# HGRN value columns as one token-major product, with three smaller edits, in a two-layer trunk on one core

## The chip, the cores and the metric

The kernel runs on one core of a Trainium2 chip. The metric is the time on the device of one execution in microseconds (us), as the median of three runs. TensorE (PE) does matrix products and transposes, VectorE (DVE) and ScalarE (ACT) work on 128 partitions, GpSimd (POOL) does some element-wise work and issues the DMAs that add while they move, and SyncE (SP) issues most other DMAs. Each engine works through its own instructions in program order and waits on semaphores.

## The reference, cut to what matters

Two trunk layers run over 128 context tokens and 512 latent tokens, 640 in all, at a model width of 2048. Per layer:

```
shift, scale, gate = split(silu(cond) @ ada_w + ada_b)      # two conditioning vectors: context, latent
h = x * (1 + scale) + shift
z = h @ w_in        # 6656 columns: aq ak av ag | hq hi hff hfb hgate | ca cb cgate
A: windowed attention with a sink (8 heads of 128, 2 key heads), gated by silu(ag)
B: HGRN2, 4 heads of 128, both directions: q = silu(hq), v = hi, k and decay from hff / hfb,
   S_t = diag(f_t) S_{t-1} + k_t v_t^T, o_t = S_t^T q_t; RMS norm, times silu(hgate)
C: conv: ca * sigmoid(cb), 31 taps over positions, LayerNorm, silu, times silu(cgate)
x = LayerNorm(ALPHA * x + gate * (concat(A, B, C) @ w_out))
```

In B, `v` enters as a matrix with the tokens on its rows: it is the stationary or the moving operand of products that contract over tokens.

## The kernel before, in words

All 640 tokens stay on the core. The modulated stream lies in SBUF with channels on partitions, as 16 blocks (k tiles) of 128 channels by 5 blocks of 128 tokens, split into a high part `HH` and a low part `HL`. Each weight tile is split the same way into `wh` (hi, lo), and every product is a sum of three: hi by HH, hi by HL, lo by HH.

**Projection tiles.** `w_in` is cut into 52 tiles of 128 columns (`NTILES`). A tile's result, 128 columns by 640 tokens, lies channel-major in two PSUM banks `z`. Per k tile and product `mm` issues two matmuls that share their weights, one over 256 tokens (L1173) and one over 384 (L1175), so a tile has 48 such pairs. Two z tiles alternate, and a tile's PSUM must be read out (`zput`) before the next tile but one may start. In the main loop PE does a tile in eight half steps, and after each `pump` lets up to three of the waiting generators (`active`) take one step; a generator that cannot get a buffer steps aside. If no z tile is free when a tile is to start, `pump_until` runs generators, one step each, and no projection matmul is issued in between.

**HGRN.** For each head four tiles come in the order hff, hfb, hi, hq. `e_hi` copies the value tile to SBUF, transposes it on PE in five blocks (`to_tokens`, L474 and L478) and copies the result to `v`, which `hg_main` reads. `hg_main` runs beside the next tiles' matmuls: its last steps are the output matmuls (L693 to L697), two copies on ACT (L699, L700), a square on ACT (L708) and on DVE (L709, L710), a column sum on PE (`psum_part`, L426 and L427), logarithm and exponential on ACT (L716, L719) and a product on DVE (L721). The four hgate tiles follow the four heads, then ak, av and four aq tiles. `e_ak` (L754, L759) reads the key tile out of PSUM as soon as it has three of the nine buffers of the pool `S`, of which `hg_main` holds up to seven.

**Modulation products.** Layer 0's shift and scale are computed on PE at the start (`ada_pe`, L317 and L327, 64 weight tiles of 512 KB); as each pair of channel blocks is ready, `build_h0` makes the stream and `start_mm` does the first three projection tiles for those two k tiles. The other four vectors (`ada_dve`) are products on DVE (L362), each of 128x256 elements against a row of the conditioning vector that is broadcast by DMA (L352); `RATE` says how often they take a step in the main loop.

**Weights in the main loop.** SP loads a weight tile (L1120); ACT writes hi (L290) and minus hi (L291), and a POOL-issued DMA adds the weights once more to give lo (L292). This is `split_add`. Elsewhere `split` does it with two instructions on ACT or POOL and on DVE or POOL.

**Between the layers.** The output projection works in column groups of 512, 512, 512, 256 and 256 (L1431; the last one L1482). For the last group the five token blocks follow one another. Each is added to the residual and normalised (`ln_norm`, half of it on ACT), and `ln_next` transposes it on PE into the next layer's stream (L1384, four banks of PSUM in turn; 16 small ACT instructions L1391 per token block). Between these stand products of layer 1's first two tiles, over the first 256 tokens.

## Time and profile before

| | |
|---|---|
| median of 3 runs | 2241.97 us (2239.75 to 2242.38) |
| profiled execution | 2247.12 us, its span 2245.3 us |
| PE busy | 2177.4 us, 97% |
| DVE busy | 1457.9 us, 65% |
| ACT busy | 1144.7 us, 51% |
| POOL busy | 601.9 us, 27% |
| DMA | 403.61 MB, 180 GB/s over the span |

PE works nearly all the time, so the span is PE's work plus the places where it stands still. The start (to about 120 us) moves data at the highest rate of the span. Layer 0's projection runs to about 930 us, its output projection to about 1140 us, the change of layers to about 1200 us, and layer 1 follows in the same order.

### The profile page before, as it was taken

Reading aid. Unit: us, or ns where it says so; the run is one execution under the profiler, and the core shown is the slowest. Engines: PE = TensorE matmul, PEld = TensorE weight load, DVE = VectorE, ACT = ScalarE, POOL = GpSimd, SP = SyncE. Lnnn points to the kernel's source line nnn. Section 1 sums busy time; section 2 is a strip of 40 time slices with the busy share of each in tenths; the row PEclk is TensorE's granted clock in tenths of the full one; section 3 lists DMA queues with packets and bytes.
Section 4 is the critical chain, followed back from the end, with each engine's and each line's share of the span. In section 5 each row is a group of like instructions: output and inputs, shape, how many; then the busy total and the mean of one; then the engine's idle time right before and its main releaser. Section 6 shows DMA issues by size and latency. Waiting matters only on the chain.

```text
span 2245.3 us, 42128 instructions
## 1 busy us (share of the span) xinstructions
PE 2177.4 (97%) x15854; PEld 2076.1 (92%) x15854; DVE 1457.9 (65%) x3799; ACT 1144.7 (51%) x2051; POOL 601.9 (27%) x690
## 2 busy tenths in 40 slices
PE   5899999999999999999989999999999999999997
PEld 2699999999999999988989999999999999998887
DVE  2478899557669999766673666543654779225457
ACT  1267877546565435511155787774555543462112
POOL 0033344332222343300032344433222123331003
PEclk9999999999999999999999999999999999999999
DMA  9978787897766888964426777778776576676333
GB/s 358 392 206 199 185 209 182 201 219 173 176 159 155 206 193 212 259 233 128 128 108 158 156 172 162 162 173 189 160 163 137 110 173 147 150 164 212 99 99 123
DMA packets 210557, 403.61 MB, mean 180 GB/s; under 512 B 24656, under 2 KB 30512, under 8 KB 209712
## 3 DMA queue, kind: packets, MB, share of 16 engines
q1 hardware_dynamic: 138992, 271.85, 38.4%
q0 software_dynamic: 61440, 116.96, 30.2%
q10 hardware_dynamic: 9920, 12.10, 1.7%
q8 instruction: 124, 2.03, 0.4%
q14 instruction: 81, 0.66, 0.1%
HBM read 383.46 MB, written 12.11 MB: 176 GB/s over the span
## 4 chain that ended last, share of the span: by engine, by line
PE 75%; DVE 9%; DMA 6%; issue 5%; ACT 3%; POOL 1%; ACTq 1%; SPq 0%; POOLq 0%; DVEq 0%
PE z L1175 29%; PE z L1173 19%; PE z L1431 9%; PE m L1431 8%; DVE junk L362 4%; DMA x<-adaw 2%; PE m L948 2%; PE m L1482 2%; PE m L862 1%; DMA s<-xT 1%; PE m L916 1%; DMA s<-s 1%; DMA wh<-win 1%; PE m L664 1%; ACT s L1391 1%
## 5 line engine op out<-in xcount | busy, mean ns | idle before, releaser
L1175 PE MATMUL z<-HH,wh 128*128 128x384 f32 x3296 | 1046.6, 339 | 0.0
L1173 PE MATMUL z<-HH,wh 128*128 128x256 f32 x3296 | 926.6, 283 | 1.9 <-DMA wh<-win 1.0
L292 POOL DMA_DIRECT2D wh<-win x388 | 345.2, 936 | 1095.3 <-ACT wh L291 1024.0
L1173 PEld LDWEIGHTS z<-HH,wh 128*128 128x128 f32 x3296 | 619.5, 189 | 5.8 <-DVE wh L287 1.6
L1175 PEld LDWEIGHTS z<-HH,wh 128*128 128x128 f32 x3296 | 620.6, 188 | 1.5
L1175 PE MATMUL z<-HL,wh 128*128 128x384 f32 x1648 | 558.2, 339 | 0.0
L362 DVE SCALAR_TENSOR_TENSOR junk<-raw,s 128x256 bf16<-128x256 f32 x1024 | 502.5, 491 | 53.2 <-DMA raw<-adawD 25.0
L1173 PE MATMUL z<-HL,wh 128*128 128x256 f32 x1648 | 461.6, 280 | 0.0
L1173 PEld LDWEIGHTS z<-HL,wh 128*128 128x128 f32 x1648 | 310.9, 189 | 0.0
L1175 PEld LDWEIGHTS z<-HL,wh 128*128 128x128 f32 x1648 | 310.4, 188 | 0.0
L291 ACT ACTIVATE wh<-wh 128x512 fp32r<-128x512 f32 x400 | 253.0, 633 | 78.5 <-PE z L1175 67.4
L290 ACT CAST wh<-raw 128x512 fp32r<-128x512 f32 x400 | 244.0, 610 | 72.0 <-issue 36.1
L286 ACT CAST wh<-raw 128x512 fp32r<-128x512 f32 x136 | 83.0, 621 | 305.0 <-PE m L1431 153.8
L1027 DVE SCALAR_TENSOR_TENSOR s<-s,sm,s 128x655 f32<-128x655 f32 x240 | 229.6, 957 | 6.3
L1431 PE MATMUL z<-wh,HH 128*128 128x512 f32 (+1 forms) x640 | 182.1, 368 | 0.0
L1431 PE MATMUL m<-wh,HH 128*128 128x512 f32 (+1 forms) x640 | 173.8, 357 | 0.0
L287 DVE TENSOR_TENSOR wh<-raw,wh 128x512 fp32r<-128x512 f32 x138 | 92.6, 687 | 119.5 <-ACT wh L286 119.5
L1431 PEld LDWEIGHTS z<-wh,HH 128*128 128x128 f32 x640 | 116.1, 189 | 20.1
L1431 PEld LDWEIGHTS m<-wh,HH 128*128 128x128 f32 x640 | 114.2, 189 | 17.6
L1431 PE MATMUL z<-wh,HL 128*128 128x512 f32 (+1 forms) x320 | 117.8, 368 | 0.0
L1431 PE MATMUL m<-wh,HL 128*128 128x512 f32 (+1 forms) x320 | 114.4, 358 | 0.0
L1096 ACT ACTIVATE s<-z 128x640 f32<-128x640 f32 x32 | 22.5, 703 | 152.5 <-PE z L1175 143.7
(561 smaller groups left out, 2718.6 us busy)
## 6 DMA issues: line engine op xcount, KB each, us to landing
raw<-win SPq DMA_DIRECT2D x416, 256.0 KB, 4.2
wh<-win POOLq DMA_DIRECT2D x388, 256.0 KB, 5.6
raw<-adawD SPq DMA_DIRECT2D x256, 256.0 KB, 4.2
x<-adaw SPq DMA_DIRECT2D x64, 512.0 KB, 8.3
raw<-wout SPq DMA_DIRECT2D x128, 256.0 KB, 2.7
s<-crow SPq DMA_DIRECT2D x32, 256.0 KB, 5.9
s<-xT ACTq DMA_DIRECT2D x16, 320.0 KB, 7.5
s<-s ACTq DMA_DIRECT2D x80, 64.0 KB, 3.9
```

The source lines that it names most:

```text
L286: act.copy(hi, src)
L287: (lo_eng or dve).tensor_tensor(lo, src, hi.bitcast(F32), op=ALU.subtract)
L290: act.copy(hi, r)
L291: act.activation(lo, hi.bitcast(F32), AF.Copy, scale=-1.0)
L292: pool.dma_start(out=lo, in_=w.bitcast(F32R), accum_op=ALU.add)
L362: dve.scalar_tensor_tensor(junk, r[:, 256 * n:256 * n + 256], 1.0, rows[0][:, 256 * c:256 * c + 256], op0=ALU.mult, op1=ALU.mult, accum_ou ...
L948: pe.matmul(o, lhsT=v_, rhs=p_, start=(y == 0 and n_ == 0), stop=(y == len(bl) - 1 and n_ == 2))
L1027: dve.scalar_tensor_tensor(acc, u[:, t:t + AW], sm[:, cw + t:cw + t + 1], acc, op0=ALU.mult, op1=ALU.add)
L1173: pe.matmul(za, lhsT=w_, rhs=h_[:, 0:2, k, :], start=st_, stop=sp_)
L1175: pe.matmul(zb, lhsT=w_, rhs=h_[:, 2:5, k, :], start=st_, stop=sp_)
L1431: pe.matmul(bs[tt][:, 0:w], lhsT=h_[:, tt, k, :], rhs=w_[:, o:o + w], start=(k == 0 and n_ == 0), stop=(k == KT - 1 and n_ == 2))
L1482: pe.matmul(b[:, 0:w], lhsT=h_[:, tt, k, :], rhs=w_[:, o:o + w], start=(k == 0 and n_ == 0), stop=(k == KT - 1 and n_ == 2))
```

## The change

Four edits. The value columns leave `NTILES`: `mm_hi` computes all 512 of them as one product with the tokens on the rows (HH and HL blocks as weights, 512 weight columns as the moving operand, five PSUM banks `G`, one for each token block; 15 matmuls per k tile), and `evac_hi` copies the five banks to where `hg_main` reads `v`. `e_hi` and its transposes go. This group is done in the place of the first tiles: in layer 0 beside `ada_pe`, in layer 1 in the change of layers, where `ln_next` has three banks in turn instead of four, and the weight tiles of the first eight k tiles are split by POOL and by `split_add` in turn. The gate tile of the head before takes the place of hi among each head's four tiles, so that hgate 3 alone stands between the last hq and ak. `ada_dve` works on 512 columns at once, with two broadcast rows per 512 that are asked for when the block begins. `conv_ln` gives one buffer back between its two sums.

```diff
-NTILES = ([(n, j) for j in range(4) for n in ("hff", "hfb", "hi", "hq")]
-          + [("hgate", j) for j in range(4)] + [("ak", 0), ("av", 0)] + [("aq", h) for h in range(4)]
+NTILES = ([(n, 0) for n in ("hff", "hfb", "hq")]
+          + [x for j in (1, 2, 3) for x in (("hff", j), ("hfb", j), ("hgate", j - 1), ("hq", j))] + [("hgate", 3)]
+          + [("ak", 0), ("av", 0)] + [("aq", h) for h in range(4)]
           + [("ak", 1), ("av", 1)] + [("aq", h) for h in range(4, 8)]
           + [(n, j) for j in range(4) for n in ("cb", "ca")]
           + [("ag", h) for h in range(8)]
           + [("cgate", j) for j in range(4)])
 NN = len(NTILES)
...
 
 ADAD = [(0, 2), (1, 1), (1, 0), (1, 2)]
-RATE = ((1.0, 0.85, 0.5, 1.2), (0.5, 0.5, 0.0, 0.8))
+RATE = ((1.05, 0.95, 0.55, 1.2), (0.5, 0.5, 0.0, 0.8))
 BLOCK = object()
...
-        rows, fly = deque(), deque()
-        tiles = [(kb, q) for kb in range(8) for q in range(8)]
-        nrow = nxt = 0
+        fly = deque()
+        tiles = [(kb, q) for kb in range(4) for q in range(KT)]
+        nxt = 0
...
-            if nrow <= kb or (nrow <= min(kb + 1, 7) and q == 4):
-                t = yield from S.get()
-                sync.dma_start(out=t[:, 0:512], in_=crow[nrow].rearrange("c k -> (c k)").partition_broadcast(P))
-                rows.append(t)
-                nrow += 1
-            yield
+            if q == 0:
+                rows = yield from S.getn(F32, F32)
+                for c in range(2):
+                    sync.dma_start(out=rows[c][:, 0:512], in_=crow[kb, c].partition_broadcast(P))
+                yield
             r = fly.popleft()
-            for n in range(2):
-                if n:
-                    yield
-                for c in range(2):
-                    o = 2 * (2 * q + n) + c
-                    dve.scalar_tensor_tensor(junk, r[:, 256 * n:256 * n + 256], 1.0, rows[0][:, 256 * c:256 * c + 256],
-                                             op0=ALU.mult, op1=ALU.mult, accum_out=aacc[:, kb, o:o + 1])
+            for c in range(2):
+                yield
+                o = 2 * q + c
+                dve.scalar_tensor_tensor(junk, r, 1.0, rows[c][:, 0:512], op0=ALU.mult, op1=ALU.mult,
+                                         accum_out=aacc[:, kb, o:o + 1])
             RAW.put(r)
-            if q == 7:
-                S.put(rows.popleft())
+            if q == KT - 1:
+                S.put(*rows)
         yield
...
-        return t["kt"], t["gg"], t["q"], t["v"]
+    def hv(l, st, j=0):
+        t = hgr[l, st][2]
+        return t["kt"], t["gg"], t["q"], mix[l, 8 + j]
...
-        yield from to_tokens(s[:, 0:T], v)
-        S.put(s)
-        flags.add(("hi", l, j))
+    def evac_hi(l, G):
+        h = outs[l][2]["h"].rearrange("p (j t) -> p j t", j=4)
+        for c in (1, 4, 0, 3, 2):
+            o, i = h[:, :, 128 * c:128 * c + 128], G[c].rearrange("p (j t) -> p j t", j=4)
+            if c > 2:
+                dve.tensor_copy(o, i)
+            else:
+                act.copy(o, i)
+        ZP.f = deque(zt)
+        M.put(mb[2])
 
     def e_hq(l, j, z):
         yield from wait(("hgset", l, j))
...
 
         total(segs)
+        S.put(r2)
...
             act.activation(acc[j][:, 0:T], mix[l, 12 + j], AF.Square)
         yield
+        r2 = yield from S.get()
         total(((slice(0, T), slice(0, T)),))
         S.put(*acc, r2)
...
 
-
-    NS = 3
-    zs = [zt[0], zt[1], (mb[2], mb[3])]
+    def mm_hi(l, G, k, tts):
+        hi, lo = wsp[l, k]
+        for tt in tts:
+            for n_, (h_, w_) in enumerate(((HH, hi), (HH, lo), (HL, hi))):
+                pe.matmul(G[tt], lhsT=h_[:, tt, k, :], rhs=w_, start=(k == 0 and n_ == 0),
+                          stop=(k == KT - 1 and n_ == 2))
+
+
+    ZP.f.clear()
     M.f = deque(mb[0:2])
-    ZP.f.clear()
+    G = [zt[0][:, 0:512], zt[0][:, 512:1024], mb[2], zt[1][:, 0:512], zt[1][:, 512:1024]]
     for k in range(6):
         load_x0(k)
+
     def start_mm(n):
-        for i in range(NS):
-            mm(0, i, zs[i], (2 * n, 2 * n + 1), (0, 1))
-            if n % 2:
-                WH.put(*wsp.pop((0, i, n // 2)))
+        for k in (2 * n, 2 * n + 1):
+            mm_hi(0, G, k, range(TT))
+            WH.put(*wsp.pop((0, k)))
 
     def after0(part, n):
         if part:
             return
         build_h0(2 * n)
         build_h0(2 * n + 1)
-        if n % 2 == 0:
-            for i in range(NS):
-                w_split(0, i, n // 2)
-        for c in range(1, 4):
-            if n == WN[c - 1]:
-                for i in range(NS):
-                    w_load1(0, i, c)
+        w_split(0, 2 * n)
+        w_split(0, 2 * n + 1)
+        w_load(0, 2 * n + 4, 2 * n + 5)
         if n == 7:
-            w_load(0, NS)
-            for c in range(4):
-                w_split(0, NS, c)
-            w_load(0, NS + 1)
+            for q in range(NG, NG + 4):
+                w_split(0, q)
+            w_load(0, *range(NG + 4, NG + 8))
         if n > 0:
             start_mm(n - 1)
...
+                o_split(l, m - NQ)
             while wnext <= m + (WLH if 0 in hold else WLA):
-                if wnext < 4 * NN:
-                    w_load1(l, wnext // 4, wnext % 4)
+                if wnext < NQ:
...
-        for i in range(first):
-            enqueue(i, zs[i] if l == 0 else zt[i])
-        for i in range(first, NN):
-            pump_until(lambda: ZP.f)
-            z = ZP.f.popleft()
+        M.f = deque(mb[3:])
+        evac_hi(l, G)
+        for i in range(NN):
+            if i == 0:
+                z = Z(mb[0], mb[1])
+            else:
+                pump_until(lambda: ZP.f)
+                z = ZP.f.popleft()
             if i == HOLD0:
                 hold.add(0)
-            rate = RATE[l][0 if i < 20 else 1 if i < 32 else 2 if i < 45 else 3]
+            rate = RATE[l][0 if i < 16 else 1 if i < 28 else 2 if i < 41 else 3]
             for c in range(4):
                 mm(l, i, z, (4 * c, 4 * c + 1), (0, 1))
                 pump(3, rate)
                 mm(l, i, z, (4 * c + 2, 4 * c + 3), (0, 1))
-                WH.put(*wsp.pop((l, i, c)))
-                ahead(i, c)
+                WH.put(*wsp.pop((l, NG + 4 * i + c)))
+                ahead(NG + 4 * i + c)
                 pump(3, rate)
             enqueue(i, z)
 
 
-        nload = wnext - 4 * NN
+        nload = wnext - NQ
...
             affine_consts()
-            w_load(l + 1, 0)
-            w_load(l + 1, 1)
-            obank = [mb[2], zh[1], zh[3], zh[1], zh[3]]
-            banks = deque(mb[3:] + mb[:3])
+            w_load(l + 1, *range(8))
+            G = [zl[0], zl[1], mb[2], zf[0], zf[1]]
+            obank = [mb[2], zl[0], zf[0], zl[0], zf[0]]
+            banks = deque(mb[3:] + mb[:2])
...
                     WH.put(*osp.pop((l, gi, k // 2)))
-                    if not last and k < 8:
-                        w_split(l + 1, 0, k // 2, pool if k // 2 in LO0 else None, pool)
+                    if not last:
+                        if k % 4 == 1:
+                            w_split(l + 1, k // 2, pool, pool)
+                        else:
+                            w_split(l + 1, k // 2, "dma")
             if last:
                 banks.append(b)
...
+                    for k in range(2):
+                        mm_hi(l + 1, G, k, range(3))
                 g = ln_next(tt - 1) if tt > 0 else iter(())
                 for _ in range(LNI):
                     next(g, None)
...
         if not last:
-            mm(l + 1, 0, zt[0], range(KT), (0,))
-            g = ln_next(TT - 1)
-            for c in range(4):
-                w_split(l + 1, 1, c, pool if c in LO1 else None, pool)
-                next(g, None)
-            next(g, None)
+            for k in range(2, 8):
+                mm_hi(l + 1, G, k, range(3))
+            for _ in ln_next(TT - 1):
+                pass
             yp.release()
             open_layer(l + 1)
-            mm(l + 1, 1, zt[1], range(KT), (0,))
-            w_load(l + 1, 2)
-            w_load(l + 1, 3)
-            for i in range(2):
-                for c in range(4):
-                    mm(l + 1, i, zt[i], range(4 * c, 4 * c + 4), (1,))
-                    WH.put(*wsp.pop((l + 1, i, c)))
-            for c in range(4):
-                w_split(l + 1, 2, c, pool if c % 2 else None)
-            ZP.f.clear()
+            for k in range(8):
+                mm_hi(l + 1, G, k, (3,))
+            nq = 8
+            for k in range(KT):
+                mm_hi(l + 1, G, k, (4,) if k < 8 else range(TT))
+                WH.put(*wsp.pop((l + 1, k)))
+                if k < 8:
+                    w_load(l + 1, nq)
+                    nq += 1
+                    w_split(l + 1, 8 + k)
+                elif k < 12:
+                    w_load(l + 1, nq)
+                    nq += 1
+                else:
+                    w_load(l + 1, nq)
+                    nq += 1
+                    w_split(l + 1, k + 4, "dma")
```

How the instructions stand now is shown at two places. The first is PE in layer 0 at the last output matmuls of head 3. `m` are PSUM banks, `z` the projection tiles, `o0h` and `h01v` hold the values. Before:

```order
L694 MATMUL m_101<-s_120,s_139 128x128
L695 MATMUL m_101<-s_3508,s_143 128x128
L697 MATMUL m_102<-s_2825,h01v 128x128
L1173 MATMUL z_99<-HH,wh_412 128x256
L1175 MATMUL z_99<-HH,wh_412 128x384
```

After, where z_99 holds the tile av 0 and z_100 has held ak 0:

```order
L687 MATMUL m_103<-s_120,s_3591 128x128
L688 MATMUL m_103<-s_137,s_117 128x128
L690 MATMUL m_101<-s_195,o0h 128x128
L434 MATMUL m_102<-s_4138,ones 128x384
L435 MATMUL m_102<-s_4139,ones 128x384
L434 MATMUL m_104<-s_4138,ones 128x256
L435 MATMUL m_104<-s_4139,ones 128x256
L1168 MATMUL z_100<-HH,wh_236 128x256
L1170 MATMUL z_100<-HH,wh_236 128x384
```

The column sum, which stood among projection matmuls, now follows the output matmuls with none in between, and the next projection matmul writes the bank that ak 0 has to leave. On ACT the same place reads, after the change:

```order
L692 COPY o0h<-m_103 128x512
L693 COPY o0h<-m_101 128x128
L701 ACTIVATE s_4138<-o0h 128x640
L709 ACT_TABLE_LOAD
L709 ACTIVATE s_195<-m_102,eps_85 128x384
L709 ACTIVATE s_195<-m_104,eps_85 128x256
L712 ACT_TABLE_LOAD
L712 ACTIVATE s_195<-s_195 128x640
L746 DMA s_120<-ckT 128x128
L747 COPY s_141<-z_100 128x128
L752 COPY s_120<-z_100 128x2x256
```

The two copies that free z_100 (L747, L752) are now the last of a chain that begins with the copies of the output; before, they stood among weight splits.

The second place is ACT in the change of layers, where `ln_next` works on the third and the fourth token block. Before:

```order
L1391 ACTIVATE s_143<-m_104,shf_83,scl_81 128x128 x4
L1391 ACTIVATE s_1973<-m_101,shf_83,scl_81 128x128 x4
L1358 ACTIVATE mv_97<-mv_97,eps_84 128x1
L1375 ACTIVATE y0y<-y0y,ats_88,mv_97 128x640
L1391 ACTIVATE s_7715<-m_102,shf_83,scl_81 128x128 x4
```

After, where the first pair of wh is the weight tile of the second k tile, and whi are the value columns:

```order
L1388 ACTIVATE s_141<-m_102,shf_83,scl_81 128x128 x4
L302 CAST wh_511<-raw_164 128x512
L303 ACTIVATE wh_514<-wh_511 128x512
L302 CAST wh_410<-raw_246 128x512
L303 ACTIVATE wh_236<-wh_410 128x512
L302 CAST wh_241<-raw_318 128x512
L303 ACTIVATE wh_7091<-wh_241 128x512
L302 CAST wh_411<-raw_244 128x512
L303 ACTIVATE wh_414<-wh_411 128x512
L1388 ACTIVATE s_6134<-m_104,shf_83,scl_81 128x128 x4
```

Four weight splits now stand between the third block's last instructions and the fourth block's first ones. On POOL the four DMAs that complete them stand between POOL's own four splits:

```order
L296 CAST wh_415<-raw_162 128x512
L299 TENSOR_TENSOR wh_510<-raw_162,wh_415 128x512
L304 DMA wh_514<-whi 128x512
L296 CAST wh_515<-raw_316 128x512
L299 TENSOR_TENSOR wh_313<-raw_316,wh_515 128x512
L304 DMA wh_236<-whi 128x512
```

Each DMA waits for its ACT instructions, and the POOL split behind it waits for the DMA's issue.

## Rows read from the trace of the kernel before

**Rows 1.** Busy time by stretch: us, PE, PEld, DVE, ACT, POOL, clock, DMA share, GB/s.

```profile
100.00:120.00 20.00, 16.81 (x183) 11.93 (x176) 9.29 (x24) 3.75 (x6) 0.00 (x0) 1.00 1.03 401
160.00:880.00 720.00, 710.11 (x5530) 703.95 (x5530) 578.46 (x1654) 431.85 (x785) 236.59 (x273) 1.00 0.79 188
1160.00:1180.00 20.00, 13.65 (x108) 12.24 (x107) 16.10 (x28) 13.83 (x38) 9.64 (x10) 1.00 0.38 133
1220.00:1940.00 720.00, 717.50 (x5614) 711.83 (x5613) 425.67 (x1022) 435.89 (x792) 241.59 (x276) 1.00 0.73 160
```

**Rows 2.** PE's timeline in the main loop: start, us, line, out<-in, count.

```profile
259.98 0.34 PE L1175 MATMUL z<-HL,wh 128*128 128x384 f32 x1
...
264.69 0.34 PE L1175 MATMUL z<-HH,wh 128*128 128x384 f32 x1
```

**Rows 3.** Chain that ended last: start, us, what.

```profile
257.95 1.78 PE m L664 x16
...
1047.24 4.08 PE z L1431 x18
```

**Rows 4.** PE's timeline at the start, with the idle time before and its releaser.

```profile
104.89 0.64 PE L317 MATMUL m<-x,s 128*32 128x256 f32 x8 [0.62 <-DMA x<-adaw]
...
117.06 0.44 PE L327 MATMUL m<-ident,s 128*128 128x128 f32 x2 [0.55 <-DVE s L323]
```

**Rows 5.** DMA issues of the page: out<-in, count, KB each, median us to landing.

```profile
wh<-win POOLq DMA_DIRECT2D x388, 256.0 KB, 5.6
...
s<-crow SPq DMA_DIRECT2D x32, 256.0 KB, 5.9
```

**Rows 6.** ACT's timeline in the change of layers.

```profile
1163.01 5.67 ACT L1391 ACTIVATE s<-m,shf,scl 128x128 f32<-128x128 f32 x16
```

**Rows 7.** Costliest groups of the page: ACT's two instructions of a weight split.

```profile
L291 ACT ACTIVATE wh<-wh 128x512 fp32r<-128x512 f32 x400 | 253.0, 633 | 78.5 <-PE z L1175 67.4
L290 ACT CAST wh<-raw 128x512 fp32r<-128x512 f32 x400 | 244.0, 610 | 72.0 <-issue 36.1
```

**Rows 8.** PE's timeline, last output matmul of head 3.

```profile
406.87 0.39 PE L697 MATMUL m<-s,h01v 128*128 128x128 f32 x2
```

**Rows 9.** ACT's timeline: end of head 3, and the reading of ak 0.

```profile
407.85 0.74 ACT L708 ACTIVATE s<-o0h 128x640 fp32r<-128x640 f32 x1
...
413.09 0.95 ACT L716 ACTIVATE s<-m,eps 128x384 f32<-128x384 f32 x2
414.06 1.28 ACT L719 ACT_TABLE_LOAD   x1
415.35 0.74 ACT L719 ACTIVATE s<-s 128x640 f32<-128x640 f32 x1
...
434.41 0.27 ACT L754 COPY s<-z 128x128 f32<-128x128 f32 x1 [7.43 <-PE z L1175]
434.58 0.59 ACT L759 COPY s<-z 128x512 f32<-128x512 f32 x1
```

**Rows 10.** DVE's timeline at the same place.

```profile
408.77 0.83 DVE L710 TENSOR_TENSOR s<-s,s 128x640 fp32r<-128x640 f32 x1
```

**Rows 11.** ACT's timeline: a table load and the instruction it is for.

```profile
1296.02 1.28 ACT L500 ACT_TABLE_LOAD   x1
1297.92 0.70 ACT L500 ACTIVATE h11q<-z 128x640 f32<-128x640 f32 x1 [0.62 <-PE z L1175]
```

**Rows 12.** PE's timeline at the start: the longest gap after the first tiles.

```profile
33.59 0.65 PE L327 MATMUL m<-ident,s 128*128 128x128 f32 x2 [3.57 <-DVE s L323]
```

**Rows 13.** Busy time by stretch after that gap, columns as in rows 1.

```profile
32.00:36.00 4.00, 2.41 (x22) 1.17 (x26) 1.87 (x5) 0.10 (x1) 0.00 (x0) 0.71 0.95 370
36.00:40.00 4.00, 3.44 (x34) 2.40 (x27) 1.57 (x5) 0.20 (x1) 0.00 (x0) 0.86 0.84 249
```

**Rows 14.** PE's timeline in the change of layers: two of its gaps.

```profile
1163.58 0.63 PE L1384 MATMUL m<-ident,y0y 128*128 128x128 f32 x4 [1.77 <-ACT s L1391]
...
1174.29 0.95 PE L1384 MATMUL m<-ident,y0y 128*128 128x128 f32 x7 [1.94 <-ACT y0y L1375]
```

More of the change, by code (lines that the diff above doesn't have):

```diff
@@ L41 @@
 NN = len(NTILES)
[L42 removed]
+NG = 16
+NQ = NG + 4 * NN
 RY = 2
```

123 lines of the change are left out of this document (52 added, 71 removed).

## Prediction

> **What bounds the kernel now.** I read the page's busy shares first, then the busy time by stretch, PE's waits, and PE's timeline where it stands still. PE is the bound: in layer 0's main loop it works 710.1 of 720 us, in layer 1's 717.5 of 720, at full granted clock [rows 1]. So a change counts in two ways only: by what it takes from PE's own work, and by the time for which PE stands still. Of that there are four places before: the start, where PE waits for DMAs, worst for the modulation weights (to 120 us, about 35 us in all); layer 0's loop (9.9 us); the change of layers (1160 to 1180: 6.35 us, and 1.0 shortly before) [rows 1, 14]; and the last 13 us, which the change leaves alone. DVE, though it works 578 us of layer 0's 720 against 426 in layer 1's [rows 1], costs PE at most the difference of their idle times, 9.9 - 2.5 = 7.4 us.
>
> **PE's own work.** In the loop, sixteen pairs of matmuls (256 and 384 tokens) take from 259.98 to 264.69, 0.2944 us a pair [rows 2]. A tile is 48 pairs, 14.1 us, four value tiles 56.5. A matmul of 512 columns with a stream block as weights, the form the new group has, takes 4.08 / 18 = 0.2267 us [rows 3], and 240 of them 54.4 us: 2.1 us less a layer. The 20 transposes of a layer go too; sixteen fp32 matmuls of that size take 1.78 us, 0.111 each [rows 3], so 2.2 us a layer, 4.4 in all.
>
> The Trainium skill ("TensorE: Matmul & The Clock Gate", Back-to-back issue gap) gives an isolated gap of columns / 2.4 ns plus 2.5 ns, so that a pair would take about 272 ns and 512 columns 216 ns, estimates by that page. By that rule the layout would save 0.4 us a layer and not 2.1, and my sum would end 3.4 us higher. The rows decide: the pair costs 8% more than the rule, the long matmul 5%.
>
> **The start of layer 0.** Three tiles were done beside the modulation, for each step of two k tiles 18 pairs, 5.3 us; now it is the whole group, 30 matmuls, 6.8 us, 1.5 more. PE's last wait for a modulation tile is at 104.89 [rows 4]; from there it works nearly without a pause through three steps of matmuls, the last two after the last transposes at 117.06. DMA is full there (share 1.03 at 401 GB/s [rows 1]), and two more weight tiles of 256 KB [rows 5] are asked for before that last tile than in the old order: 0.52 MB, 1.3 us. So the group ends 1.3 + 3 x 1.5 = 5.8 us later than the three tiles did, but one tile of 14.1 us more is done: 8.3 us gained, the layout's 2.1 among them. If PE were the bound in all eight steps it would be 14.1 - 12 = 2.1; if only the last two counted, 11.1.
>
> **The wait for ak 0, new.** As the order shows, a single gate tile and ak 0 and av 0 follow the last hq, where four gate tiles did. ak 0 can't be read out while `hg_main` of head 3 holds the buffers, so both z tiles are full, and PE must run through the end of head 3 with nothing beside it. The chain from the last output matmul (406.87, PE free at about 407.1 [rows 8]): two copies on ACT, then the square begins at 407.85 [rows 9]; DVE's difference ends at 409.60 [rows 10]; four column-sum matmuls of about 0.15 us, the first half ready at about 410.2 and the second 0.3 later; two logarithms 0.95, a table load 1.28, the exponential 0.65 until the next can begin, the two copies of ak 0 0.76 [rows 9], and some 0.2 for a DMA issue and hand-overs: about 414.3. The logarithm's own table load is hidden, since a load goes ahead of the wait of its instruction (1296.02, while the activation starts at 1297.92, after PE) [rows 11]. PE stands still 414.3 - 407.1 less 0.6 of column sums, 6.6 us, in each layer: 13.2. If the first load isn't hidden it is 7.9 each; if ACT and DVE run shorter by half a microsecond in places, 5.5. Before, all this lay beside projection matmuls. Behind the waiting matmul on PE stands tile aq 0, whose weights are ready; nothing else is late because of it.
>
> **The change of layers.** The first two k tiles' products for three token blocks come before `ln_next` of the fourth block. The second k tile's weights are split by `split_add`; its two ACT instructions stand behind the third block's last ones. Those are the first half of the row that starts at 1163.01, 16 x 0.354 us long [rows 6], and end at 1165.8, or some 1.7 us earlier if POOL disturbs DVE less; then 0.61 + 0.63 us [rows 7] and a DMA that lands 5.6 us after issue [rows 5]: 1171.0 to 1172.7. PE had finished the last group's products at 1161.8 (1163.58 less the 1.77 of waiting [rows 14]); with three banks in turn instead of four I take 1.4 us of bank waits more, and nine products of the first k tile, 2.0 us, so it arrives at 1165.3. It waits about 6.5 us. After that 54 products of 0.2267 us, 12.2 us, lie ahead of the last block's transposes, so the gap of 1.94 before them and the 1.77 before the fourth block's [rows 14] go, with the smaller ones. Idle after: 6.5 and about 4.0 of bank waits (1.0 before, 1.4 more ahead of the fourth block, 1.6 for the banks of the last two), 10.5 against 7.35; less the layout's 2.1: 1.0 us lost. At best, with no wait left, 9.5 gained; at worst, if the later split DMAs are late in turn too, 6 lost.
>
> **The clock.** After PE's gap of 3.57 us at 33.59 [rows 12] the granted clock read 0.71 and 0.86 in the next two stretches of 4 us [rows 13]: part of each at 1.2 GHz instead of 2.4. 0.29 x 4 + 0.14 x 4 = 1.7 us of full-speed work lost. The gaps under 2 us in the change of layers left it at 1.00 [rows 1]. The change makes three longer gaps; two with that price: 3.4 us. None 0, all 5.1.
>
> The Trainium skill (same page, HAM oscillation) says that idle gaps between bursts of matmuls bring the clock to half, and that each return is paid again. By it all three would pay, and the sum would end 1.7 us higher; rows 12 and 13 show it for one gap.
>
> **Wide products, buffer, gate tiles.** 512 products on 512 columns instead of 1024 on 256 save DVE fixed costs, but only idle time of PE counts, at most 7.4 us gained. Against it, the two broadcast rows were asked for half a block early and now are asked for as the block starts, two steps ahead, with 5.9 us to landing [rows 5]: DVE's queue, with head work behind it, can stop for two or three us, and four blocks a vector fall on about three heads in layer 0, up to 6 us lost. I take 0. The buffer given back and the other gate tiles change no wait of PE: 0, within that range.
>
> **Sum.** -4.4 (transposes) - 8.3 (start) + 13.2 (ak 0) + 1.0 (layers) + 3.4 (clock) = +4.9 us on 2247.1, the profiled execution, which is 5.2 above the median of 2241.97. So 2247 us as a median.
>
> **Rivals.** (1) *The change of layers closes.* If the second k tile's split lands when PE arrives, which speaks for itself if POOL's issue comes by 1160 and not 1165, PE has 16 us of products to cover both normalisations, 2 us of idle are left, and the layers give 7.5 where I lose 1.0; with one gap less the clock costs 1.7 less. 4.9 - 8.5 - 1.7 = -5.3: 2237. For it: the 12.2 us of cover are real. Against it: the place of the four splits in ACT's order. (2) *The clock stays up* through the new waits: 2243.5. For it: column sums of 0.6 us break the gap, and 1.8 us gaps did nothing. (3) *The rows of the wide products are late* and stop heads 0 to 2: +6, 2253. For it: two steps are about 3.5 us of PE's time, less than 5.9; against it, DVE itself runs behind PE there. (4) *The wait for ak 0 is not there*, because something else lies beside the chain: 13.2 and the clock's 3.4 go, 2230. The order speaks against it.
>
> **How the numbers follow.** Within 0.2% (4.5 us) a measurement of this kernel can't tell from no change: 2237.5 to 2246.5. The forecast 0.38, rival 1 0.22, rival 2 0.20, rival 3 0.15, rival 4 0.05. The forecast lies just above the bound, so a third of it counts as no change; rival 1 is half faster and half no change. Slower: 0.25 + 0.15 and 0.05 of rival 2, 0.45; faster 0.11 + 0.05 and 0.04 from gains I priced low, 0.20; the same 0.35. The range, 2236 to 2256, takes in rivals 1 to 3. Of the likeliest alone: 2242 to 2252.
>
> **What would show it.** In the changed profile: a PE gap or two of together 6 to 7 us per layer between the output matmuls of head 3 and the first matmul of aq 0, ended by ACT's copies of ak 0; a gap of about 6 us in the change of layers that ends with a DMA of value weights; clocks under 1.00 behind them; the first main-loop tile about 5.8 us later than the fourth tile started before. If the heads' compact matmuls (L540) wait longer than before, rival 3 is there. I'm wrong if PE runs through at aq 0, or if the start ends as late as 12 us after before.

## The result, and the profile after

The changed kernel takes 2257.30 us (median of 4 runs, 2255.96 to 2258.11) against 2241.49 of the kernel before: ratio 1.0073, 95% interval 1.0061 to 1.0085, so 15.8 us slower. I had forecast 2247 and a range that ended at 2256. Its profiled execution took 2257.82 us (span 2255.9), 10.7 more than that of before. One execution of e12 below (2390.68 us, at a granted clock of 0.85) fell in a slower state of the chip, and its median is that of the other eleven.

Three of the stretches of [rows 1] in the changed kernel (PE, PEld, DVE, ACT, POOL busy, granted clock, DMA share, GB/s):

```profile
160.00:880.00 720.00, 699.60 (x5429) 690.91 (x5428) 548.34 (x1116) 427.43 (x775) 244.45 (x272) 0.99 0.78 185
1160.00:1180.00 20.00, 15.02 (x87) 13.04 (x86) 8.31 (x17) 11.89 (x29) 11.52 (x13) 0.83 0.45 99
1220.00:1940.00 720.00, 710.18 (x5505) 700.85 (x5504) 408.58 (x781) 432.58 (x782) 237.94 (x270) 1.00 0.70 154
```

DVE works 30 us less in layer 0's loop than in [rows 1], and yet PE stands still 20.4 us instead of 9.9; in layer 1's it stands still 9.8 instead of 2.5. PE's timeline in order of time: a wait at the second head's early products (L566), three at ak 0 in layer 0, one at the first attention products, one in the change of layers, three at ak 0 in layer 1 (in brackets the idle time before and its releaser):

```profile
254.00 0.80 PE L566 MATMUL m<-s,s 128*64 128x64 f32 x20 [1.44 <-DVE s L527]
...
439.99 0.44 PE L434 MATMUL m<-s,ones 128*128 128x384 f32 x1 [1.39 <-ACT s L701]
441.00 0.69 PE L435 MATMUL m<-s,ones 128*128 128x384 f32 x1 [0.57 <-DVE s L703]
446.74 0.58 PE L1168 MATMUL z<-HH,wh 128*128 128x256 f32 x1 [4.63 <-ACT s L752]
...
528.27 0.44 PE L855 MATMUL m<-a00k,a00qa 128*128 128x384 f32 x1 [2.78 <-DVE ats L870]
...
1173.01 0.79 PE L1176 MATMUL z<-wh,HH 128*128 128x512 f32 x1 [4.47 <-DMA wh<-whi]
...
1533.52 0.44 PE L434 MATMUL m<-s,ones 128*128 128x384 f32 x1 [1.39 <-ACT s L701]
1534.53 0.44 PE L435 MATMUL m<-s,ones 128*128 128x384 f32 x1 [0.57 <-DVE s L703]
1540.03 0.58 PE L1168 MATMUL z<-HH,wh 128*128 128x256 f32 x1 [4.83 <-ACT s L752]
```

The seven at ak 0 and in the change of layers are those that the prediction named; the other two it did not. Five stretches of the loops and of the change of layers run partly at the lower of the two clocks (1.2 GHz instead of 2.4), each behind one of these waits, or behind one of 1.52 us that ends at 277.07 (the same columns as in the windows above):

```profile
276.00:280.00 4.00, 2.93 (x48) 2.87 (x49) 3.93 (x8) 3.94 (x12) 1.73 (x2) 0.62 0.94 191
280.00:284.00 4.00, 4.00 (x27) 4.00 (x27) 4.00 (x10) 3.92 (x6) 2.60 (x5) 0.95 0.98 246
440.00:444.00 4.00, 1.54 (x4) 0.99 (x4) 0.85 (x2) 2.23 (x3) 0.00 (x0) 0.60 0.00 0
444.00:448.00 4.00, 1.26 (x5) 1.26 (x6) 1.50 (x3) 2.66 (x5) 0.89 (x1) 0.50 0.06 16
448.00:452.00 4.00, 4.00 (x20) 4.00 (x18) 0.28 (x1) 1.84 (x3) 1.75 (x3) 0.62 0.60 155
528.00:532.00 4.00, 3.73 (x17) 3.73 (x18) 3.21 (x11) 3.52 (x8) 0.86 (x1) 0.69 0.82 176
532.00:536.00 4.00, 4.00 (x26) 4.00 (x26) 3.86 (x15) 2.21 (x6) 0.15 (x2) 0.88 0.79 159
1172.00:1176.00 4.00, 2.99 (x7) 2.41 (x8) 0.00 (x0) 0.16 (x1) 3.92 (x5) 0.50 0.54 85
1176.00:1180.00 4.00, 3.49 (x19) 2.94 (x19) 0.69 (x2) 2.26 (x7) 2.09 (x3) 0.74 0.71 99
1540.00:1544.00 4.00, 3.97 (x17) 3.97 (x18) 0.26 (x1) 1.31 (x3) 2.07 (x2) 0.59 0.32 82
```

Busy time times missing clock: 1.3, 2.8, 1.6, 2.4 and 1.6 us of full-speed work lost, 9.7 in all.

### The profile page after: what moved, and what is told of

The parts are those of the page before. It is cut to its first block, busy times and chain, and to the rows that moved or that the text cites. A ratio compares the mean times of both kernels' runs of the same rounds, so it can differ in the third digit from the quotient of the medians.

```text
span 2255.9 us, 40430 instructions
## 1 busy us (share of the span) xinstructions
PE 2177.9 (97%) x15526; PEld 2054.6 (91%) x15526; DVE 1376.0 (61%) x2785; ACT 1133.1 (50%) x2030; POOL 597.6 (26%) x680
## 4 chain that ended last, share of the span: by engine, by line
PE 76%; issue 6%; DVE 6%; DMA 5%; ACT 4%; POOL 2%; ACTq 0%; SPq 0%; POOLq 0%; DVEq 0%
PE z L1170 26%; PE z L1168 17%; PE z L1428 9%; PE m L1428 8%; PE z L1176 4%; DVE junk L370 2%; PE m L941 2%; PE m L855 2%; PE m L1479 2%; DMA s<-crow 1%; DMA raw<-adawD 1%; DMA x<-adaw 1%; PE m L328 1%; PE m L909 1%; PE m L1176 1%
## 5 line engine op out<-in xcount | busy, mean ns | idle before, releaser
L1170 PE MATMUL z<-HH,wh 128*128 128x384 f32 x3008 | 960.0, 339 | 0.0
L1168 PE MATMUL z<-HH,wh 128*128 128x256 f32 x3008 | 850.2, 283 | 9.5 <-ACT s L752 9.5
L304 POOL DMA_DIRECT2D wh<-win x380 | 338.0, 938 | 1106.3 <-ACT wh L303 1047.3
L1168 PEld LDWEIGHTS z<-HH,wh 128*128 128x128 f32 x3008 | 567.7, 189 | 12.9 <-ACT s L752 10.0
L1170 PEld LDWEIGHTS z<-HH,wh 128*128 128x128 f32 x3008 | 567.5, 189 | 1.5
L1170 PE MATMUL z<-HL,wh 128*128 128x384 f32 x1504 | 509.9, 339 | 0.0
L370 DVE SCALAR_TENSOR_TENSOR junk<-raw,s 128x512 bf16<-128x512 f32 x512 | 406.9, 795 | 63.1 <-DMA raw<-adawD 33.8
L1168 PE MATMUL z<-HL,wh 128*128 128x256 f32 x1504 | 421.3, 280 | 0.0
L1168 PEld LDWEIGHTS z<-HL,wh 128*128 128x128 f32 x1504 | 283.9, 189 | 0.0
L1170 PEld LDWEIGHTS z<-HL,wh 128*128 128x128 f32 x1504 | 283.7, 189 | 0.0
L1176 PE MATMUL z<-wh,HH 128*128 128x512 f32 x256 | 81.8, 401 | 4.5 <-DMA wh<-whi 4.5
```

The source lines that it names most:

```text
L304: pool.dma_start(out=lo, in_=w.bitcast(F32R), accum_op=ALU.add)
L370: dve.scalar_tensor_tensor(junk, r, 1.0, rows[c][:, 0:512], op0=ALU.mult, op1=ALU.mult, accum_out=aacc[:, kb, o:o + 1])
L1168: pe.matmul(za, lhsT=w_, rhs=h_[:, 0:2, k, :], start=st_, stop=sp_)
L1170: pe.matmul(zb, lhsT=w_, rhs=h_[:, 2:5, k, :], start=st_, stop=sp_)
L1176: pe.matmul(G[tt], lhsT=h_[:, tt, k, :], rhs=w_, start=(k == 0 and n_ == 0), stop=(k == KT - 1 and n_ == 2))
```

## Experiments

Theory: the wait for ak 0, the change of layers and the clock behind them make the loss. Rivals: the waits of the heads on DVE, the wide products, the place and the engine of the gate products. A slot is a buffer of the pool `S`; the pace is `RATE`, how often the modulation products take a step. Each ratio is to the kernel before, run beside it on the same chip. e1, e2, e5, e8, e11 and e14 change one thing of the changed kernel, e3 the package of the modulation products.

**e1, gate tile 2 later.**
```
-  hff 3, hfb 3, hgate 2, hq 3, hgate 3, ak 0
+  hff 3, hfb 3, hq 3, hgate 2, hgate 3, ak 0
```


> The changed kernel with one edit: gate tile 2 stands behind the last query tile of the heads, so that two single tiles and not one lie between it and ak 0. Theory A (the wait for ak 0 is there because the buffer-bound end of head 3 has too few tiles beside it): PE's stretches of 6.6 and 6.8 us before aq 0 go in both layers, and with them the half-speed stretches behind them (2.8 and 1.7 us of work); 17 to 18 us faster than the changed kernel, about 2240, ratio to the kernel before 0.999. Rival B (head 3 is bound by its own chain of DVE and ACT, whatever stands beside it; head 2 has then lost a tile of cover): the same idle time reappears as waits of the heads' own products on DVE, L561 to L600, and the time stays within 4 us of 2257, ratio 1.005 to 1.009.

2253.37 us, ratio 1.0055 [1.0042, 1.0067]: 3.9 faster, not 17. The wait before aq 0 is gone in both layers, as theory A says, but most of its time comes back as rival B says. PE at head 3's first products, and DVE's and ACT's timelines there:

```profile
382.72 1.62 PE L562 MATMUL m<-s,s 128*128 128x128 f32 x6 [2.82 <-ACT wh L304]
...
1477.34 2.12 PE L562 MATMUL m<-s,s 128*128 128x128 f32 x10 [2.84 <-ACT wh L304]
```
```profile
375.89 1.28 ACT L710 ACT_TABLE_LOAD   x1
...
378.15 1.28 ACT L713 ACT_TABLE_LOAD   x1
379.44 0.74 ACT L713 ACTIVATE s<-s 128x640 f32<-128x640 f32 x1
...
380.22 0.88 DVE L715 SCALAR_TENSOR_TENSOR o0h<-o0h,sm,s 128x640 f32<-128x640 f32 x1 [6.03 <-ACT s L713]
...
381.75 0.82 DVE L528 SCALAR_TENSOR_TENSOR s<-s,h01q 128x640 f32<-128x640 f32 x1
```

Head 3 now starts the moment head 2 lets go. Its level products stand on DVE behind head 2's last product (L715), and that waits 6 us for ACT's logarithm and exponential with a table load ahead of each. The page names an ACT split as PE's releaser; PE starts when L528 ends (382.57).

**e2, POOL first in the change of layers.**
```
-  if k % 4 == 1:              # POOL splits tiles 0, 2, 4, 6
+  if k in (1, 3, 5, 9, 13):   # POOL splits tiles 0, 1, 2, 4, 6
```


> The changed kernel with one edit: in the change of layers the first three value-weight tiles are split by POOL, and the first split that ends in a DMA is that of the fourth. Theory A (the 4.5 us wait there is for the DMA of the second tile, and the half-speed stretch behind it costs 2.7 us more): the gap falls to under 1 us, the granted clock stays at 1.00, 6 to 7 us faster than the changed kernel, about 2251, ratio 1.004. Rival B (the wait only moves: the fourth tile's DMA, or the fourth token block's normalisation, is as late): a gap of 3 us or more stays within 15 us of it, and the time changes by under 2 us, ratio 1.006 to 1.008.

2250.77 us, ratio 1.0044 [1.0031, 1.0058]: 6.5 faster, as theory A says. The wait is gone, the largest left there is 0.89 us, and the clock stays at full speed (PE's window at that place):

```profile
1168.00:1172.00 4.00, 3.11 (x23) 2.61 (x22) 2.45 (x6) 3.97 (x11) 3.83 (x6) 1.00 0.62 74
```

**e3, narrow products.** Products of 256 columns, rows half a block early, pace 1.0, 0.85, 0.5, all as before:
```
-  STT(junk, r, 1.0, rows[c][:, 0:512], ...)
+  STT(junk, r[:, 256*n:256*n+256], 1.0, rows[0][:, 256*c:256*c+256], ...)
```


> The changed kernel with the modulation products as before: 256 columns each, the row of the next block asked for half a block early, and the pace of them as before. Theory A (the wide products' late rows and their longer turns on DVE are what the heads of layer 0 and the first attention products wait for): of layer 0's 13.8 us of idle time outside the wait at ak 0 some 4 us go, and the half-speed stretch at 276 us (1.7 us); 4 to 6 us faster than the changed kernel, ratio 1.005. Rival B (DVE's long turns beside POOL make these waits, in either form): no change within 2 us, ratio 1.007. Rival C (wide products do help, because they take 96 us less of DVE): 4 us or more slower, ratio 1.009 or above.

2268.60 us, ratio 1.0122 [1.0109, 1.0136]: 11.3 slower, rival C. PE now waits 7 to 8 us at the first products of each of heads 1 to 3 in layer 0, 22.7 in all. Head 1, PE and DVE:

```profile
261.81 0.48 PE L569 MATMUL m<-s,s 128*64 128x64 f32 x4 [4.87 <-DVE s L530]
```
```profile
248.70 3.28 DVE L373 SCALAR_TENSOR_TENSOR junk<-raw,s 128x256 bf16<-128x256 f32 x1
...
255.86 5.89 DVE L530 SCALAR_TENSOR_TENSOR s<-s,h01q 128x640 f32<-128x640 f32 x1
```

L530 takes 0.81 us elsewhere; why it takes 5.89 here comes with e5.

The 11.3 are a balance, for the wait at ak 0 is gone in both layers: ACT reads ak 0 (L750) 25 us before it copies head 3's output (L695), where in the changed kernel it does so at the end of the head.

```profile
1532.67 0.24 ACT L750 COPY s<-z 128x128 f32<-128x128 f32 x1
...
1557.69 0.59 ACT L695 COPY o1h<-m 128x512 f32<-128x512 f32 x1 [4.29 <-PE m L691]
```

The order of the tiles is that of the changed kernel, and in layer 1 the pace is too. The rows of the conditioning vector differ. Counted along the kernels' order of instructions, when ak 0 comes up head 3 holds three of the nine buffers of `S`, the gate tile one, the cached keys one, and the rows two, with narrow products one: two are free, or the three that `e_ak` needs. So the second row of the wide products is a part of the cause of that wait. No run has the wide products with one buffer more.

**e4, the kernel before once more.** No edit.

> The kernel before, unchanged, taken once more with a profile. The profiled execution of the kernel before stood 5.2 us above the median of its runs, that of the changed kernel 0.5 above. Theory A (a chance of that one execution: a stretch at half speed or late DMAs): the new profile shows a span near 2240 and one of its idle stretches at the start, in the heads or the attention is shorter by some 5 us. Rival B (a profile costs this kernel 5 us each time): the span is again near 2245 and the waits are the same to half a microsecond. Ratio 1.000 either way.

Ratio 0.9998 [0.9990, 1.0007], and a span of 2238.8 us in the profile against 2245.3: theory A. The last transposes of the start come 2.6 us earlier (114.46 against 117.06, [rows 4]), and layer 0's loop has no wait at the first attention products. A window of e4 over the first attention products, then the same place in the first profile of before:

```profile
510.00:526.00 16.00, 16.00 (x113) 15.71 (x111) 11.34 (x40) 8.26 (x19) 3.89 (x4) 1.00 0.69 149
```
```profile
525.05 0.58 PE L862 MATMUL m<-a00k,a00qa 128*128 128x384 f32 x1 [2.21 <-DVE ats L877]
```
```profile
516.00:532.00 16.00, 13.79 (x87) 13.55 (x86) 12.63 (x41) 9.64 (x22) 3.88 (x4) 0.89 0.71 156
```

The profile that the prediction rests on was thus an unlucky execution: 2.6 us at the start, 2.2 at this wait and some 1.5 of clock (13.79 x 0.11) are that one run's, 6.3 of the 6.5. Later the two differ both ways: in the change of layers and in layer 1 e4 stands still 2.2 us less, but pays 2.9 us of clock in the change of layers, where the first profile paid none.

**e5, gate products on DVE.**
```
-  eng = dve if k >= 14 else pool
+  eng = dve if k >= 14 or 8 <= k < 12 else pool
```


> The changed kernel with one edit: the product of a head's gate runs on DVE, not on POOL. In the changed kernel it stands on POOL right ahead of the next head's first subtractions (238.53, 2.04 us; they start at 241.65), and DVE's own products stretch to 4.2 us meanwhile, so that PE waits for DVE before the products of levels 64 and 32 (0.4 and 1.4 us at 250.8 and 252.6, and so at each head); before, no head waited there. Theory A (the gate product between two heads makes these waits): the waits at levels 64 and 32 go in layer 0 (4.0 us in all), a clock stretch with them; 3 to 6 us faster than the changed kernel, about 2253, ratio 1.005. Rival B (DVE itself is the late one, and 0.8 us more on it makes the waits longer): the same or up to 3 us slower, ratio 1.007 to 1.009.

2251.15 us, ratio 1.0046 [1.0034, 1.0059]: 6.1 faster, theory A. In the changed kernel, at the start of head 1, POOL (L1098 is the gate product, L514 and L517 the head's subtractions) and DVE:

```profile
238.53 2.04 POOL L1098 TENSOR_TENSOR o0h<-o0h,s 128x640 f32<-128x640 f32 x1
...
241.65 1.90 POOL L514 TENSOR_TENSOR s<-h01gg 128x640 f32<-128x640 f32 x1
242.87 1.91 POOL L517 TENSOR_TENSOR s<-h01gg 128x640 f32<-128x640 f32 x1
...
247.62 1.55 POOL L514 TENSOR_TENSOR s<-h01gg 128x640 f32<-128x640 f32 x1
248.84 1.60 POOL L517 TENSOR_TENSOR s<-h01gg 128x640 f32<-128x640 f32 x1
...
241.16 4.19 DVE L370 SCALAR_TENSOR_TENSOR junk<-raw,s 128x512 bf16<-128x512 f32 x1
245.38 0.69 DVE L370 SCALAR_TENSOR_TENSOR junk<-raw,s 128x512 bf16<-128x512 f32 x1
...
247.47 3.65 DVE L527 SCALAR_TENSOR_TENSOR s<-s,h01q 128x640 f32<-128x640 f32 x1
```

A DVE instruction of 0.69 us that meets POOL's first pair of subtractions takes 4.19, and L527, 0.82 us elsewhere, meets the second pair and takes 3.65. Each ends 0.6 to 0.7 us, about its own length, after POOL's pair. In e3, L530 lasted through four such subtractions. The Trainium skill ("SBUF — State Buffer", SBUF: two separate sides) says that a DVE instruction with two SBUF inputs and a POOL instruction that reads SBUF need the same pair of ports, that one holds it for its whole length, and that the other blocks. The rows agree in the blocking; that DVE waits out several POOL instructions in a row, they alone show. So POOL's work at a head's start holds DVE up too. With the gate product on DVE (0.83 us there), L527 comes 1.6 us before POOL's second pair, which now meets a modulation product; it takes 0.81, and PE has no wait at levels 64 and 32:

```profile
238.63 0.83 DVE L1098 TENSOR_TENSOR o0h<-o0h,s 128x640 f32<-128x640 f32 x1
...
247.01 0.81 DVE L527 SCALAR_TENSOR_TENSOR s<-s,h01q 128x640 f32<-128x640 f32 x1
```

**e6, the edits of e1, e2 and e5 together.**

> Three edits together: gate tile 2 behind the last query tile, the first three value-weight tiles split by POOL in the change of layers, the gate products of the heads on DVE. If the three causes are separate, their gains add: 3.9 + 6.5 measured alone, and 3 to 6 expected of the third: 2241 to 2244, ratio 1.000 to 1.001. If they overlap (the head that follows without a pause waits for the former head's last product on DVE whatever POOL does): 2246 to 2248, ratio 1.002 to 1.003.

2239.58 us, ratio 0.9996 [0.9987, 1.0005]. 3.9 + 6.5 + 6.1 = 16.5 alone, 17.7 together: the gains add, so the three causes are separate.

**e7, the kernel before with wide products alone,** and **e9, with their whole package** (wide, the pace of the changed kernel, and the conv's slot):
```
   total(segs)
+  S.put(r2)
...
+  r2 = yield from S.get()
   total(((slice(0, T), slice(0, T)),))
```


> The kernel before with the wide modulation products alone (512 columns, both rows asked for as a block starts); nothing else of the change. In the changed kernel, taking them away cost 11 us. Theory A (they only repay what the change itself costs the heads, since before PE waits for DVE 8 us in all of layer 0's loop): within 4 us of the kernel before, ratio 0.998 to 1.002. Rival B (DVE's time is worth as much there): 8 us or more faster, ratio 0.996 or below. Rival C (the rows asked for late stop heads that had no wait): 4 us or more slower, ratio 1.002 or above.

> The kernel before with the whole package around the wide products: 512 columns, the pace of the changed kernel (1.05, 0.95, 0.55), and the sum slot of the conv given back; value tiles and gate tiles as before. The wide products alone cost 76 us there: PE stood still from about 915 to 992 while DVE worked off products at 0.74 us each, since the two rows that a block holds left the conv's normalisation too few slots. Theory A (the slot given back is what makes the wide products possible; without that stall they are neutral or a little better in the heads): the stall goes; 2236 to 2242, ratio 0.998 to 1.0005. Rival B (the two rows starve the conv in any case): the stall stays at 20 us or more, ratio 1.01 or above.

e7: 2317.03 us, ratio 1.0335 [1.0320, 1.0349], rival C, and worse than it said. e9: 2240.92, ratio 0.9994 [0.9986, 1.0003], theory A. Alone, the wide products hold two slots through a block, and the order waits for the conv's sums until the block is through; which of the two other edits of the package lifts that, e11 shows.

**e8, gate tiles last,** as before: hff, hfb, hq for each head, then hgate 0 to 3.

> The changed kernel with the four gate tiles of the heads behind the last query tile, as before; three single tiles a head. Theory A (the gate tiles' place is what costs: their products between the heads, and the missing cover at ak 0): the wait at ak 0 goes, so do the waits at levels 64 and 32, and it is 15 us or more faster than the changed kernel, 2242 or less, ratio 1.000. Rival B (a head needs the emission steps of nearly four tiles; with three, each head starts the moment the former lets go, its first products wait as head 3's did in the run with gate tile 2 late, 2.8 us): the ak 0 wait goes, but three waits of 2 to 3 us a layer come at heads 1 to 3, with clock stretches: about the same as with gate tile 2 late, 2250 to 2256, ratio 1.004 to 1.007.

2275.82 us, ratio 1.0156 [1.0142, 1.0170]: 18.5 slower, worse than either theory. The wait at ak 0 goes, but now heads 1 and 2 start as head 3 did in e1, and PE waits twice 8 us for DVE in each layer (PE's and DVE's timeline at head 1):

```profile
245.12 1.12 PE L566 MATMUL m<-s,s 128*64 128x64 f32 x16 [7.96 <-DVE s L527]
```
```profile
242.62 0.89 DVE L714 SCALAR_TENSOR_TENSOR o0h<-o0h,sm,s 128x640 f32<-128x640 f32 x1 [8.43 <-ACT s L712]
```

So with the single value tiles gone, the gate tiles are what keeps the heads apart: where one is taken away (e1) or all (e8), the next head starts too early.

**e11, the conv's slot kept** in the changed kernel (e7's missing edit, undone here).

> The changed kernel with the sum slot of the conv kept through both passes, as before; all else of the change in place. The prediction priced the slot given back at nothing. Theory A (with the two rows of the wide products the conv's normalisation finds no slots until a block of products is through): PE stands still for 50 to 80 us near the end of layer 0's loop, time 2305 to 2335, ratio 1.02 to 1.035. Rival B (the slot matters only in the kernel before, where the pace of the products is another): no change, 2257, ratio 1.007.

2322.31 us, ratio 1.0357 [1.0340, 1.0375]: theory A. DVE works off modulation products, PE stands still:

```profile
920.00:960.00 40.00, 0.00 (x0) 0.00 (x0) 34.89 (x101) 0.00 (x0) 0.00 (x0) 0.51 0.63 179
```

**e10, e6 with head 3 two steps and av one step later,** and **e12, e10 with a lower pace:**
```
+  for _ in range(2 if j == 3 else 0): yield      # e10: after head 3 has its lock
-  RATE = ((1.05, 0.95, 0.55, 1.2), ...)
+  RATE = ((1.05, 0.75, 0.75, 1.2), ...)          # e12
```


> The three edits together, and two more: head 3 starts two emission steps later (in the run of the three edits its first products wait 2.8 us in each layer, behind the former head's last product on DVE), and the transposes of av one step later (they wait 1.0 and 2.2 us for ACT's copy). Theory A (these waits are a matter of distance in the order, and 3.5 us more of projection products cover them): the four waits go, 8.8 us in all, with two or three clock stretches of 1.7 us; 8 to 13 us faster than the three edits, 2228 to 2232, ratio 0.994 to 0.996. Rival B (the end of head 3 then comes too late for ak 0, av 0 and aq 0): a new wait of 3 us or more before aq 0, no gain, ratio 0.998 to 1.001.

> As the run with head 3 later, and the pace of layer 0's modulation products is 0.75 in the attention's tiles and 0.75 in the conv's (from 0.95 and 0.55). In the runs of the changed kernel PE waits 2.8 us and twice 0.9 us for DVE in the first attention products of layer 0, with a clock stretch. Theory A (the modulation products on DVE make these waits): they fall by half, 2 to 4 us faster than that run, ratio 0.993 to 0.995. Rival B (they come from the order of the attention's own steps): no change within 1.5 us, or slower because the conv is now disturbed.

e10: 2250.37 us, ratio 1.0036 [1.0024, 1.0048], 10.8 slower than e6: a miss for both theories. Instead of 2.8 us, head 3 waits at four of its products in layer 0 (1.65, 1.81, 0.95 and 1.44 us), and in layer 1 at four too, once long:

```profile
1491.34 0.71 PE L536 MATMUL m<-s,s 128*32 128x32 f32 x40 [4.02 <-DVE s L530]
```

PE's idle time is 4.5 us more than in e6 in layer 0 and 5.1 more in layer 1. Why DVE is late there by more than the two steps is open. e12: 2242.75, ratio 1.0000 [0.9991, 1.0009], 7.6 faster than e10 by the pace, more than theory A's 2 to 4.

**e13, e6 with the pace of e12,** and **e14, the changed kernel with that pace alone.**

> The three edits that added up (gate tile 2 behind the last query tile, POOL first in the change of layers, gate products on DVE) and the pace of layer 0's modulation products of 0.75 in the attention's and in the conv's tiles; head 3 and av as in the changed kernel. Theory A (the modulation products on DVE make PE wait in the first attention products, 4.7 us and a clock stretch of 1.7 in the run of the three edits, and their pace is a separate cause): 2 to 6 us faster than the three edits, 2234 to 2238, ratio 0.997 to 0.9985. Rival B (what the pace brought in the run with head 3 later was that run's own late end of head 3): within 1.5 us of the three edits, ratio 0.999 to 1.0005.

> The changed kernel with the pace alone edited, to 0.75 and 0.75. Theory A (pace is a separate cause of the loss): 2 to 6 us faster than the changed kernel, 2251 to 2255, ratio 1.005 to 1.0065; the wait for ak 0 stays at 6.6 us in each layer. Rival B: 2257, ratio 1.007, or slower because more products fall on the conv.

e13: 2231.18 us, ratio 0.9961 [0.9947, 0.9975], 8.4 faster than e6 and faster than both kernels, more than theory A's 2 to 6. Of the 8.2 us between the two profiles 4.6 lie in layer 0's loop, where the pace acts; the rest lies where the two kernels do the same, and is not the pace's. e14: 2252.60, ratio 1.0044 [1.0032, 1.0057], 4.7 faster than the changed kernel: theory A. The stretch of the first attention products, in e14, and the wait left in e13:

```profile
480.00:560.00 80.00, 80.00 (x548) 78.91 (x547) 52.62 (x146) 45.07 (x107) 22.75 (x24) 1.00 0.78 182
```
```profile
515.46 0.44 PE L856 MATMUL m<-a00k,a00qa 128*128 128x384 f32 x1 [0.85 <-DVE ats L871]
```

**e15, e9 with the same pace:** the wide products without the token-major group.

> The kernel before with the package around the wide products (wide, slot given back) and the pace of 0.75 and 0.75; value tiles, gate tiles and change of layers as before. The mended changed kernel took 2231.2. Theory A (what is gained over the kernel before comes from the token-major group at the start and in the layout, 8.7 and 2.2 a layer; wide products and pace only take away waits that the group's kernel has): 2238 to 2242, ratio 0.9985 to 1.000. Rival B (wide products and the pace make the gain, and the group is worth little after its waits): 2230 to 2235, ratio 0.995 to 0.997.

2239.07 us, ratio 0.9989 [0.9980, 0.9998]: theory A. With its waits mended, the group is worth 7.9 us by the medians of e13 and e15, or 6.3 by their ratios, whose intervals leave some 4 us either way; pace and package give 2.2 without it.

## Why the prediction was wrong

Slower was right; the size was not. The step that failed is the zero for the wide products, the buffer and the gate tiles; the clock was sized too small beside it. The terms, the profile after against the two profiles of before:

| term | predicted | against the first | against e4 |
|---|---|---|---|
| transposes | -4.4 | -4.4, taken over | -4.4, taken over |
| start | -8.3 | -11.3 | -8.7 |
| wait for ak 0 | +13.2 | +13.4 | +13.4 |
| change of layers | +1.0 | -1.5 | -0.3 |
| clock | +3.4 | +8.2 | +6.8 |
| wide products, buffer, gate tiles | 0 | +4.4 of idle time | +6.9 of idle time |
| sum | +4.9 | +8.8, of 10.7 | +13.7, of 17.1 |

- *Transposes and layout.* Neither is seen by itself; the measured columns take over the -4.4, and in the change of layers the layout's 2.1. What the sums miss is mostly this: PE's busy time less the clock's loss falls by 3.9 us in layer 1 (2.9 against e4), where the sum has 4.3, and in layer 0's loop, one tile aside, by 0.5, where it has 2.2.
- *Start.* The first main-loop tile begins at 130.75, the fourth tile before at 127.90: 2.85 later, not 5.8, and 14.1 less to do. Against e4 (125.30) it is 5.45 later and 8.7 gained; the step was sized well, the first profile's start was slow.
- *Wait for ak 0.* It is there in place and order: 1.39 + 0.57 + 4.63 us in layer 0, 1.39 + 0.57 + 4.83 in layer 1, ended by ACT's copy of ak 0. That the size fits is in part luck. The table load of the logarithm is not hidden as [rows 11] had it: it begins when the first column sums are done, in both layers.

```profile
441.76 1.28 ACT L709 ACT_TABLE_LOAD   x1 [1.83 <-PE m L435]
443.06 0.94 ACT L709 ACTIVATE s<-m,eps 128x384 f32<-128x384 f32 x2
```

  So the chain lasts 8.1 and 7.9 us and not 7.2, but PE's column sums inside it, in layer 0 at the lower clock, take 1.55 and 1.1 us and not 0.6. The cause was half seen: the forecast gave the wait to the order of the tiles, and e3 shows it gone in that order with one row less in `S`. Nor can it simply be bought back: e1 puts one tile there and gets 3.9.
- *Change of layers.* The wait is on the DMA of k tile 1, 4.47 us and not 6.5; six gaps make 7.9 us instead of 10.5. ACT came to the split at 1167.34, behind the third block's rows as forecast, and POOL issued the DMA at 1168.95. In e2 this wait and the 2.4 us of clock behind it go, and the time falls by 6.5.
- *Clock: the step that failed by size.* I priced two gaps at 1.7 us. All three long ones paid, by 2.8, 2.4 and 1.6 us, and two shorter ones in the heads and the attention did too (1.3 and 1.6). That is 9.7, less 1.5 that the first profile of before paid in the attention, or 2.9 that e4 paid in the change of layers. The Trainium skill ("TensorE: Matmul & The Clock Gate", HAM oscillation) has idle gaps between bursts bring the clock down and each return paid again, which I had weighed and discounted by 1.7; the rows of the three long gaps agree with it.
- *Wide products, buffer, gate tiles: the step that failed by cause.* "The buffer given back and the other gate tiles change no wait of PE: 0" was wrong in every part. The gate tiles put a POOL product between two heads (6.1 us, e5). The raised pace puts modulation products on DVE in the first attention products (4.7, e14). The second row of the wide products leaves ak 0 one buffer short (e3). Against these the wide products give 11.3 back in the balance (e3, with the pace of before), and the slot that I priced at nothing is worth 65 (e11). The nothing was a sum of large terms of both signs.
- *Rival 3.* The late rows are there (DVE waits 2.10 us for one at 268.28, PE 1.52 behind it), but the sign that the prediction named is not: the compact matmuls (L540, now L533) wait 4.3 us in layer 0 and not longer than the 7.7 of before. The new waits are at levels 64 and 32 (4.8 us, none before) and in the first attention products (4.4; 2.2 in the first profile, none in e4).
- *From profile to median.* The medians lie 15.8 us apart, the first two profiles 10.7: e4 shows that the first profile of before was slow by chance, and the changed kernel's profile stands 0.5 above its median. The forecast put its +4.9 on the median, so this cost it little, but it hid 2.5 us of the heads' waits and made the start look better than it was. Against e4 the sum falls short by 12.2: heads 6.9, clock 3.4 and 3.4 not placed by a row of the table, less 1.5 for the other terms.

## What to carry to other kernels

A work item that serves as cover is worth more than its own time: taking four value tiles out of the loop saved at the start what was forecast, and the heads then met each other on ACT, DVE and POOL. Before an off-path edit is priced at nothing, look at what stands behind it in its engine's order and at who is left short by the buffers that it holds. A term that comes out right can do so by two errors; check its chain row by row. And a sum worked against one profiled execution carries that execution's chance waits: compare its span with the other runs, and don't pass the difference on.

## Of the hardware, not expected

- In the changed kernel a wait of 4.47 us and one of 1.52 were both followed by a stretch at the lower clock; waits of 1.77 and 1.94 in the first profile of before were not [rows 1, 14], while in e4 one of 1.79 in the same place was (PE's windows):

```profile
1156.00:1160.00 4.00, 2.15 (x14) 1.64 (x15) 2.87 (x3) 4.00 (x11) 3.84 (x4) 0.82 0.51 211
1160.00:1164.00 4.00, 4.00 (x28) 4.00 (x27) 3.90 (x7) 2.42 (x7) 3.61 (x5) 0.75 0.13 51
```

  The same program thus pays for a short gap in one execution and not in the next. A wait of 1.44 us that the changed kernel has at 254.00 without a loss is followed in e2 (1.44 at 254.05) by clocks of 0.74 and 0.83 over the windows from 252 to 260.
- A DVE product of 0.69 to 0.82 us lasts 3.7 to 5.9 beside two to four of POOL's tensor instructions, and the trace shows it as busy, not as waiting: a busy share of DVE holds waits for POOL.
